# Six Winograd pairs instead of five per down projection, with two of four weight sums made by accumulating DMAs

## The chip, the cores and the metric

The kernel runs on one core of a Trainium2 chip. The metric is device time in microseconds, of one launch that does the whole computation; the median of several runs counts. TensorE (PE) multiplies, VectorE (DVE) and ScalarE (ACT) prepare operands and do the pointwise work, GpSimd (POOL) does little, and SyncE (SP) only issues DMAs.

## The reference, cut to what matters

The model is a two-layer trunk over 256 tokens of width 1024, all in float32. Each layer is a feed-forward block (FFN), a mixer and a second FFN, each followed by a residual and a layer norm, so four FFNs in all. The change sits in the FFN:

```python
def swiglu(x, w_gu, w_down):
    g, u = jnp.split(x @ w_gu, 2, axis=-1)          # 1024 -> 2 x 2816
    return (jax.nn.silu(g) * u) @ w_down            # 2816 -> 1024
...
x = layer_norm(ALPHA * x + 0.5 * swiglu(x, w_gu, w_down), g, b)
```

The hidden width 2816 is 22 chunks of 128. The down projection is therefore a sum of 22 products, each of a 256x128 piece of the hidden state and 128 rows of `w_down`.

## The kernel before, in words

**Precision.** Every float32 operand is split into a rounded part (`hi`) and a remainder (`lo`); a product is three matmuls (`mm3`, lines 169 to 171): hi*hi, hi*lo, lo*hi. The split is one copy on ACT (line 141) and one subtraction on DVE (line 142).

**Weight stream.** All weights come as one list `W` of tiles of 128x1024 floats (512 KB), in the order of use. SP loads them in that order into `raw`, a ring of RAW = 5 buffers (`w_dma`). `refill` splits the next tile when the ring of RING = 8 hi/lo slots has room, and then issues one more load; a slot comes free when the last matmul that reads it is done (`w_done`). So the load of tile n+5 waits until tile n is split, and the split of a tile waits for a slot that PE frees. SP issues in program order; on the other engines a scheduler orders the instructions at build time, by priority and by its own estimate of when operands are there.

**The FFN.** Up to eight tiles ("groups") and then, chunk by chunk, a `gate` and an `up` tile give the hidden state: `chunk(c)` makes silu(gate)*up in PSUM banks of tag `m` (three buffers) and splits the result. A plain hidden chunk is multiplied at the end by its `down` tile in `out_proj` (24 matmuls of 512 columns for two chunks). Ten of the chunks (C0 = 4 and on, NP = 5 pairs) go another way: two chunks, two token halves and two column halves make a 2x2 block product, which a Strassen-Winograd scheme does in seven products instead of eight. For output half r and pair p, `pair(r, p)` does these seven (21 matmuls of 256 columns) into four PSUM accumulators of tag `a`; `fold(r)` combines the four into the residual `xn` when the last pair of the half is done. The scheme needs sums of hidden blocks (`hs`, lines 407 to 410) and four sums of weight blocks (`tt`), which DVE makes from the raw tile in `refill` (lines 124, 126, 127) before they are split like a weight tile. A pair tile takes two slots.

**Order.** `SLOTS` says after which chunk a pair comes. With five pairs, half r = 0 comes after chunks 7, 9, 11, 13 and 15, and r = 1 after chunks 16, 17, 18, 19 and 20; then chunk 21, then `out_proj` with 12 plain down tiles. `out_proj` takes its four accumulators from tag `a`, does the first five chunks for both token halves and the last seven in a skewed order, so that the layer norm of token half 0 runs beside the matmuls of half 1.

**The rest.** The layer norm's gain and bias lie in a buffer `gb` of their own, which `load_gb` fills on SP when the layer norm before has used it up. Intermediates live in `page`, a pool of PAGES = 30 buffers of 516 floats.

Of the kernel before, what the change touches and what calls it, by code (L numbers as in the profile page):

```python
# [11 lines left out]
OP = mybir.AluOpType  # L12
# [10 lines left out]
EPS = 1e-5  # L23
RING = 8
RAW = 5
PAGES = 30
NP = 5
C0 = 4
NWARM = 7
TT = 2  # L30


PAIRS = range(C0, C0 + 2 * NP, 2)
# [1 line left out]
SLOTS = {}  # L35
for _p in range(NP):
    SLOTS.setdefault(C0 + 2 * _p + 3, []).append((0, _p))
    SLOTS.setdefault(C0 + 2 * NP + 2 + _p, []).append((1, _p))


def ffn_plan(head):
# [8 lines left out]
def trunk(ctx, tc, W, F_d, x_d, g_d, b_d, rope_d, id_d, idb_d, mk_d, tri_d, sel_d,  # L50
# [16 lines left out]
    def bank_a(shape=(P, 512)):  # L67
        return bank("a", 4, shape)
# [18 lines left out]
    def small(name, shape):  # L87
        return spool.tile(list(shape), F32, tag=name, name=name)

    raw, whi, wlo = {}, {}, {}  # L90
    stream = {}
    for n0, head in ((0, 1), (94, 2), (160, 2), (258, 2)):
        for i, e in enumerate(ffn_plan(head)):
# [7 lines left out]
    def w_dma():  # L101
        n = ring["dma"]
        if n < NG:
            raw[n] = wpool.tile([P, 1024], F32, tag="raw", name="raw", bufs=RAW)
            nc.sync.dma_start(out=raw[n], in_=W[n - 4])
            ring["dma"] = n + 1

    def slot():
        ring["free"] -= 1
# [3 lines left out]
    def refill():  # L113
        while ring["split"] < NG and ring["free"] >= (2 if paired(ring["split"]) else 1):
            n = ring["split"]
            ring["split"] = n + 1
            r = raw.pop(n)
            hi, lo = slot()
            if paired(n):
                yh, yl = slot()  # L120
                tt = wpool.tile([P, 4, 256], F32, tag="tt", name="tt", bufs=TT)
                bb = r.rearrange("p (a n) -> p a n", a=4)
                sub = nc.vector.tensor_tensor
                sub(out=tt[:, 0:2, :], in0=bb[:, 0:1, :].to_broadcast([P, 2, 256]), in1=bb[:, 1:3, :], op=OP.subtract)
                split(r[:, 256:1024], hi[:, 0:768], lo[:, 0:768])
                sub(out=tt[:, 2, :], in0=bb[:, 2, :], in1=tt[:, 0, :], op=OP.subtract)
                sub(out=tt[:, 3, :], in0=bb[:, 3, :], in1=tt[:, 2, :], op=OP.subtract)
                split(tt.rearrange("p a n -> p (a n)"), yh, yl)
                whi[n], wlo[n] = (hi, yh), (lo, yl)
            else:  # L130
                split(r, hi, lo)
                whi[n], wlo[n] = hi, lo
            w_dma()
# [39 lines left out]
    xTh = cpool.tile([P, KC, S], F32R, name="xTh")  # L173
    xTl = cpool.tile([P, KC, S], F32R, name="xTl")
    xn = cpool.tile([P, 2, D], F32, name="xn")
    gb = cpool.tile([P, 2, D], F32, name="gb")
    ident = cpool.tile([P, P], F32, name="ident")
    identb = cpool.tile([P, P], BF, name="identb")
    maskb = cpool.tile([P, 2, P], BF, name="maskb")
# [18 lines left out]
                                               ap=[[0, P], [1, width]]))  # L198

    def load_gb(k):  # L200
        bcast(gb[:, 0, :], g_d, k, D)
        bcast(gb[:, 1, :], b_d, k, D)

    st = {}

# [30 lines left out]
            nc.sync.dma_start(out=ident, in_=id_d)  # L236
    refill()
    nc.sync.dma_start(out=xn, in_=x_d)
    load_gb(0)

    def load_consts():
        nc.sync.dma_start(out=identb, in_=idb_d)
# [9 lines left out]
        nc.gpsimd.tensor_tensor(out=r, in0=r, in1=half[:, :width], op=OP.pow)  # L252
        return r

    def layer_norm(t, acc, scale, eps, k, last=False, segs=((0, 512), (512, 512))):
        st = small("lnst", [P, 3, 6])
        mv = small("lnmv", [P, 2])
        for i, (o, w) in enumerate(segs):
            if i < 2:
                sl = xn[:, t, i * 512:(i + 1) * 512]  # L260
                if scale is None:
                    nc.vector.tensor_tensor(out=sl, in0=sl, in1=acc[i], op=OP.add)
                else:
                    nc.vector.scalar_tensor_tensor(out=sl, in0=sl, scalar=scale, in1=acc[i], op0=OP.mult, op1=OP.add)
            else:
                sl = xn[:, t, o:o + w]
                nc.vector.tensor_tensor(out=sl, in0=sl, in1=acc[2][:, 0:w], op=OP.add)
            nc.vector.bn_stats(out=st[:, i, :], in_=xn[:, t, o:o + w])
            yield 1 + min(i, 1)
        nc.vector.bn_aggr(out=mv, in_=st[:, 0:len(segs), :])  # L270
        rs = rstd_of(mv[:, 1:2], eps, "lnrs")
        for h in range(2):
            sl = xn[:, t, h * 512:(h + 1) * 512]
            nc.vector.scalar_tensor_tensor(out=sl, in0=sl, scalar=mv[:, 0:1], in1=gb[:, 0, h * 512:(h + 1) * 512],
                                           op0=OP.subtract, op1=OP.mult)
        for h in range(2):
            sl = xn[:, t, h * 512:(h + 1) * 512]
            nc.vector.scalar_tensor_tensor(out=sl, in0=sl, scalar=rs, in1=gb[:, 1, h * 512:(h + 1) * 512],
                                           op0=OP.mult, op1=OP.add)
            yield 1  # L280
            if last:
                nc.sync.dma_start(out=out_d[t * P:(t + 1) * P, h * 512:(h + 1) * 512], in_=sl)
            else:
                pt = bank_a((P, 4, P))
                for c in range(4):
                    nc.tensor.transpose(pt[:, c, :], sl[:, c * P:(c + 1) * P], ident)  # L286
                o = (slice(None), slice(4 * h, 4 * h + 4), slice(t * P, (t + 1) * P))
                split(pt, xTh[o], xTl[o])
            yield 1
        if t == 1 and k + 1 < 6:  # L290
            load_gb(k + 1)

    pending = []

# [21 lines left out]
        w_done(n)  # L316
        tick()

    def out_proj(nk, n0, lhs, skew, k, scale, eps, last):
        acc = [[None, None], [None, None]]  # L320

        def one(c, t, release, hs=(0, 1)):
            n = n0 + c
            lh, ll = lhs(c, t)
            for h in hs:
                if acc[t][h] is None:
                    acc[t][h] = bank_a()
            for h in hs:
                mm3(acc[t][h], lh, ll, whi[n][:, h * 512:(h + 1) * 512], wlo[n][:, h * 512:(h + 1) * 512],
                    c == 0, c == nk - 1)  # L330
            if release:
                w_done(n)
            if 1 in hs:
                tick()

        for c in range(nk - skew):
            one(c, 0, False)
            one(c, 1, True)
        for c in range(nk - skew, nk):
            one(c, 0, False, (0,))  # L340
        ln0 = layer_norm(0, acc[0], scale, eps, k, last)
        next(ln0)
        for c in range(nk - skew, nk):
            one(c, 0, False, (1,))
        spawn(ln0)
        if last:
            segs = ((0, 512), (512, 256), (768, 256))
            accs = [acc[1][0], acc[1][1], bank_m()]
            ln1 = layer_norm(1, accs, scale, eps, k, last, segs)
            for i, (o, w) in enumerate(segs):  # L350
                for c in range(nk - skew, nk):
                    n = n0 + c
                    lh, ll = lhs(c, 1)
                    mm3(accs[i][:, 0:w], lh, ll, whi[n][:, o:o + w], wlo[n][:, o:o + w],
                        i == 2 and c == nk - skew, c == nk - 1)
                next(ln1)
            finish(ln0)
            return spawn(ln1)
        for c in range(nk - skew, nk):
            one(c, 1, True)  # L360
        finish(ln0)
        return spawn(layer_norm(1, acc[1], scale, eps, k, last))

    def ffn(n0, k, ln_prev, last=False):
        hT, hS, acc = {}, {}, {}
# [17 lines left out]
        def chunk(c):  # L383
# [20 lines left out]
                                    op=OP.mult)  # L404
            if o == 1:
                tt = nc.vector.tensor_tensor
                tt(out=hs[:, 4, :], in0=hs[:, 0, :], in1=hs[:, 2, :], op=OP.add)
                tt(out=hs[:, 5, :], in0=hs[:, 4, :], in1=hs[:, 1, :], op=OP.subtract)
                tt(out=hs[:, 6, :], in0=hs[:, 0, :], in1=hs[:, 1, :], op=OP.subtract)
                tt(out=hs[:, 7, :], in0=hs[:, 3, :], in1=hs[:, 5, :], op=OP.subtract)  # L410
                for lo, hi in ((1, 5), (5, 8)):
                    qh = page("hSh", [P, hi - lo, P], F32R)
                    ql = page("hSl", [P, hi - lo, P], F32R)
# [4 lines left out]
        def pair(r, p):  # L418
# [18 lines left out]
        def fold(r, a):  # L437
# [8 lines left out]
            tt(out=u[:, 1, :], in0=u[:, 0, :], in1=a[3][:, 0, :], op=OP.add)  # L446
            tt(out=x[:, 1, :], in0=u[:, 0, :], in1=a[1][:, 1, :], op=OP.add)
# [431 lines left out]
def _arrays(np, i):  # L879
# [5 lines left out]
    def ffn(l, f, head):  # L885
# [4 lines left out]
        for e in ffn_plan(head):  # L890
# [93 lines left out]
```

## Time and profile before

| | |
|---|---|
| median of 3 runs | 958.51 us (958.47 to 958.96) |
| the profiled execution's own time | 959.6 us |
| its span, first to last instruction | 957.9 us |
| PE / DVE / ACT / POOL busy, share of the span | 99% / 76% / 52% / 2% |
| mean granted TensorE clock | 0.998 of full |
| DMA: moved, mean rate | 183.09 MB, 191 GB/s |

The time of the profiled execution is 1.7 us more than its span, and 1.1 us more than the median. A matmul's shown duration includes the pipeline and overlaps the next one; what a matmul costs is the distance from its start to the next start.

### The profile page before, as it was taken

The page shows a single profiled execution, that of the slowest core. Times are in us where ns is not written, and L with a number is a line of the kernel's source. Part 1 is how long each engine was busy: PE and PEld are TensorE (multiplying, and loading weights), DVE is VectorE, ACT ScalarE, POOL GpSimd, SP SyncE. Part 2 cuts the span into 40 slices and gives each one's busy share as a digit, 9 for nine tenths or more (in the row PEclk, how much of TensorE's full clock was granted, in tenths as well). Part 3 has the DMA queues.
Part 4 walks back from the last instruction along what each step waited for, and adds up shares of the span by engine and source line. Part 5 has one row for each costly group of instructions (what it writes and reads, how often), then busy time and mean ns, then how long its engine had stood idle before and what let it go on. Part 6 is the DMA issues. An engine that isn't in the chain of part 4 may idle for free.

```text
span 957.9 us, 16624 instructions
## 1 busy us (share of the span) xinstructions
PE 946.4 (99%) x6586; PEld 867.2 (91%) x6586; DVE 732.5 (76%) x1125; ACT 495.6 (52%) x705; POOL 21.0 (2%) x28
## 2 busy tenths in 40 slices
PE   9999999999999999999999999999999999999997
PEld 7999998887888999998889999988888789999985
DVE  7698886685767788976878779748767887888765
ACT  6565564445645555553355555525675445555530
POOL 0000000010100000000000000001000000000000
PEclk9999999999999999999999999999999999999999
DMA  8976557474436665576565656756634366655631
GB/s 307 319 237 217 174 200 228 161 273 152 138 129 219 202 195 176 179 234 205 173 221 162 190 177 200 238 158 221 220 132 122 136 213 216 195 173 180 219 112 44
DMA packets 52077, 183.09 MB, mean 191 GB/s; under 512 B 6176, under 2 KB 6688, under 8 KB 51872
## 3 DMA queue, kind: packets, MB, share of 16 engines
q1 hardware_dynamic: 51856, 181.77, 57.6%
q8 instruction: 51, 0.84, 0.4%
q10 hardware_dynamic: 144, 0.26, 0.1%
q14 instruction: 26, 0.21, 0.1%
HBM read 180.97 MB, written 1.05 MB: 190 GB/s over the span
## 4 chain that ended last, share of the span: by engine, by line
PE 70%; DVE 2%; DMA 1%; issue 1%; ACT 1%; POOL 0%; DVEq 0%
PE ps_m L169 15%; PE ps_m L170 15%; PE ps_m L171 15%; PE ps_a L169 5%; PE ps_a L170 5%; PE ps_a L171 5%; PE ps_a L430 3%; PE ps_a L431 3%; PE ps_a L429 3%; DVE wlo L142 1%; PE ps_a L286 1%; DMA raw<-in_W 1%; ACT whi L141 0%; PE ps_t L377 0%; PE ps_a L613 0%
## 5 line engine op out<-in xcount | busy, mean ns | idle before, releaser
L141 ACT CAST whi<-raw 128x1024 fp32r<-128x1024 f32 (+2 forms) x327 | 331.0, 1016 | 258.9 <-PE ps_a L171 77.2
L142 DVE TENSOR_TENSOR wlo<-raw,whi 128x1024 fp32r<-128x1024 f32 (+2 forms) x327 | 380.9, 1176 | 89.2 <-ACT whi L141 86.4
L169 PE MATMUL ps_m<-xTh,whi 128*128 128x256 f32 x1280 | 358.8, 280 | 0.9 <-DVE qkc L760 0.9
L171 PE MATMUL ps_m<-xTh,wlo 128*128 128x256 f32 x1280 | 357.9, 280 | 0.2 <-DVE wlo L142 0.2
L170 PE MATMUL ps_m<-xTl,whi 128*128 128x256 f32 x1280 | 357.7, 279 | 0.0
L169 PEld LDWEIGHTS ps_m<-xTh,whi 128*128 128x128 f32 x1280 | 240.6, 188 | 1.5 <-issue 1.2
L170 PEld LDWEIGHTS ps_m<-xTl,whi 128*128 128x128 f32 x1280 | 240.6, 188 | 0.6 <-issue 0.3
L171 PEld LDWEIGHTS ps_m<-xTh,wlo 128*128 128x128 f32 x1280 | 240.5, 188 | 0.6 <-DVE wlo L142 0.4
L169 PE MATMUL ps_m<-whi,xTh 128*128 128x512 f32 x224 | 90.9, 406 | 0.0
L170 PE MATMUL ps_m<-wlo,xTh 128*128 128x512 f32 x224 | 89.3, 399 | 0.0
L171 PE MATMUL ps_m<-whi,xTl 128*128 128x512 f32 x224 | 88.8, 397 | 0.0
L430 PE MATMUL ps_a<-wlo,hSh 128*128 128x256 f32 x280 | 78.8, 281 | 0.0
L429 PE MATMUL ps_a<-whi,hSh 128*128 128x256 f32 x280 | 78.8, 281 | 0.0
L431 PE MATMUL ps_a<-whi,hSl 128*128 128x256 f32 x280 | 78.8, 281 | 0.0
L169 PE MATMUL ps_a<-whi,hT 128*128 128x512 f32 (+1 forms) x192 | 75.3, 392 | 0.0
L170 PE MATMUL ps_a<-wlo,hT 128*128 128x512 f32 (+1 forms) x192 | 75.0, 390 | 0.0
L171 PE MATMUL ps_a<-whi,hT 128*128 128x512 f32 (+1 forms) x192 | 74.9, 390 | 0.0
L141 ACT CAST whi<-tt 128x1024 fp32r<-128x1024 f32 x40 | 42.1, 1052 | 42.6 <-issue 18.3
L430 PEld LDWEIGHTS ps_a<-wlo,hSh 128*128 128x128 f32 x280 | 52.8, 189 | 0.0
L431 PEld LDWEIGHTS ps_a<-whi,hSl 128*128 128x128 f32 x280 | 52.8, 188 | 0.0
L429 PEld LDWEIGHTS ps_a<-whi,hSh 128*128 128x128 f32 x280 | 52.7, 188 | 0.0
L142 DVE TENSOR_TENSOR wlo<-tt,whi 128x1024 fp32r<-128x1024 f32 x40 | 48.8, 1221 | 3.4 <-ACT whi L141 3.4
(224 smaller groups left out, 1013.7 us busy)
## 6 DMA issues: line engine op xcount, KB each, us to landing
raw<-in_W SPq DMA_DIRECT2D x320, 512.0 KB, 4.4
gb<-in_g SPq DMA_DIRECT2D x6, 512.0 KB, 4.2
gb<-in_b SPq DMA_DIRECT2D x6, 512.0 KB, 5.2
raw<-in_F SPq DMA_DIRECT2D x7, 384.0 KB, 4.0
xn<-in_x SPq DMA_DIRECT2D x1, 1024.0 KB
out<-xn SPq DMA_DIRECT2D x4, 256.0 KB, 2.0
swt<-in_sw SPq DMA_DIRECT2D x2, 256.0 KB, 6.7
hg<-in_hg SPq DMA_DIRECT2D x2, 256.0 KB, 5.5
```

The costliest lines, as they stand in the source:

```text
L141: nc.scalar.copy(out=hi, in_=src)
L142: nc.vector.tensor_tensor(out=lo, in0=src, in1=hi.bitcast(F32), op=OP.subtract)
L169: mm_(out=out, lhsT=lh, rhs=rh, start=start, stop=False)
L170: mm_(out=out, lhsT=lh, rhs=rl, start=False, stop=False)
L171: mm_(out=out, lhsT=ll, rhs=rh, start=False, stop=stop)
L286: nc.tensor.transpose(pt[:, c, :], sl[:, c * P:(c + 1) * P], ident)
L429: mm_(out=o, lhsT=lh, rhs=rh, start=p == 0 and h == 0, stop=False, skip_group_check=True)
L430: mm_(out=o, lhsT=lh, rhs=rl, start=False, stop=False, skip_group_check=True)
L431: mm_(out=o, lhsT=ll, rhs=rh, start=False, stop=p == NP - 1, skip_group_check=True)
```

## The change

NP goes from 5 to 6, so two more chunks (14 and 15) leave the plain down projection: 12 pair tiles and 10 down tiles per FFN instead of 10 and 12. Half r = 0 now comes after chunks 7, 9, 11, 13, 15 and 17, and half r = 1 after 18, 19 and 20 and, three pairs in a row, after 21. The signs of the Winograd scheme are arranged anew so that two of the four weight sums are plain additions to a first block. A pair tile is no longer one load: SP loads two blocks into `tt`, SP loads three blocks into `raw`, and GpSimd issues a transfer that adds the fourth block from HBM onto both blocks in `tt`. DVE makes only the other two sums. `out_proj` of an FFN takes three accumulators from tag `m` and one from tag `t` (one buffer). The buffer `gb` goes; gain and bias lie in four pages that `out_proj` loads at its start; PAGES goes to 32 and the ring of `tt` from 2 to 3.

```diff
-PAGES = 30
-NP = 5
+PAGES = 32
+NP = 6
-TT = 2
+TT = 3
...
-    SLOTS.setdefault(C0 + 2 * NP + 2 + _p, []).append((1, _p))
+    SLOTS.setdefault(min(C0 + 2 * NP + 2 + _p, FC - 1), []).append((1, _p))
...
     def w_dma():
...
-            raw[n] = wpool.tile([P, 1024], F32, tag="raw", name="raw", bufs=RAW)
-            nc.sync.dma_start(out=raw[n], in_=W[n - 4])
             ring["dma"] = n + 1
+            r = raw[n] = wpool.tile([P, 1024], F32, tag="raw", name="raw", bufs=RAW)
+            w = W[n - 4]
+            if not paired(n):
+                nc.sync.dma_start(out=r, in_=w)
+                return
+            tt = sums[n] = wpool.tile([P, 4, 256], F32, tag="tt", name="tt", bufs=TT)
+            nc.sync.dma_start(out=tt[:, 0:2, :].rearrange("p a n -> p (a n)"), in_=w[:, 0:512])
+            nc.sync.dma_start(out=r[:, 0:768], in_=w[:, 0:768])
+            nc.gpsimd.dma_start(out=tt[:, 0:2, :], in_=w[:, None, 768:1024].to_broadcast([P, 2, 256]), accum_op=OP.add)
...
             if paired(n):
                 yh, yl = slot()
-                tt = wpool.tile([P, 4, 256], F32, tag="tt", name="tt", bufs=TT)
-                bb = r.rearrange("p (a n) -> p a n", a=4)
-                sub = nc.vector.tensor_tensor
-                sub(out=tt[:, 0:2, :], in0=bb[:, 0:1, :].to_broadcast([P, 2, 256]), in1=bb[:, 1:3, :], op=OP.subtract)
-                split(r[:, 256:1024], hi[:, 0:768], lo[:, 0:768])
-                sub(out=tt[:, 2, :], in0=bb[:, 2, :], in1=tt[:, 0, :], op=OP.subtract)
-                sub(out=tt[:, 3, :], in0=bb[:, 3, :], in1=tt[:, 2, :], op=OP.subtract)
+                tt = sums.pop(n)
+                split(r[:, 0:768], hi[:, 0:768], lo[:, 0:768])
+                add = nc.vector.tensor_tensor
+                add(out=tt[:, 2, :], in0=r[:, 256:512], in1=tt[:, 0, :], op=OP.add)
+                add(out=tt[:, 3, :], in0=r[:, 512:768], in1=tt[:, 2, :], op=OP.add)
                 split(tt.rearrange("p a n -> p (a n)"), yh, yl)
...
     def load_gb(k):
-        bcast(gb[:, 0, :], g_d, k, D)
-        bcast(gb[:, 1, :], b_d, k, D)
+        gb = {}
+        for h in range(2):
+            for j, d in enumerate((g_d, b_d)):
+                v = gb[j, h] = page("gb", [P, 512])
+                nc.sync.dma_start(out=v, in_=bass.AP(tensor=d.tensor, offset=d.offset + k * D + h * 512,
+                                                     ap=[[0, P], [1, 512]]))
+        return gb
...
-        if t == 1 and k + 1 < 6:
-            load_gb(k + 1)
...
     def out_proj(nk, n0, lhs, skew, k, scale, eps, last, banks=None):
         acc = [[None, None], [None, None]]
+        gb = load_gb(k)
+        if banks is None:
+            banks = {(t, h): bank_a for t in range(2) for h in range(2)}
...
-                tt(out=hs[:, 4, :], in0=hs[:, 0, :], in1=hs[:, 2, :], op=OP.add)
-                tt(out=hs[:, 5, :], in0=hs[:, 4, :], in1=hs[:, 1, :], op=OP.subtract)
-                tt(out=hs[:, 6, :], in0=hs[:, 0, :], in1=hs[:, 1, :], op=OP.subtract)
-                tt(out=hs[:, 7, :], in0=hs[:, 3, :], in1=hs[:, 5, :], op=OP.subtract)
+                tt(out=hs[:, 4:6, :], in0=hs[:, 0:1, :].to_broadcast([P, 2, P]), in1=hs[:, 1:3, :], op=OP.subtract)
+                tt(out=hs[:, 6, :], in0=hs[:, 5, :], in1=hs[:, 1, :], op=OP.subtract)
+                tt(out=hs[:, 7, :], in0=hs[:, 3, :], in1=hs[:, 6, :], op=OP.add)
...
-        return out_proj(len(PLAIN), at["down", PLAIN[0]], lhs, 7, k, None, 4.0 * EPS, last)
+        return out_proj(len(PLAIN), at["down", PLAIN[0]], lhs, 7, k, None, 4.0 * EPS, last,
+                        {(0, 0): bank_m, (0, 1): bank_m, (1, 0): bank_m, (1, 1): bank_t})
```

In `pair` three of the seven products take other weight columns, and `fold` makes its sums with the new signs, the last addition to token half 0 as two instructions of 256 columns instead of one of 512.

## Rows read from the trace of the kernel before

**Rows 1.** The page: busy time by engine, and the chain by engine.
```profile
PE 946.4 (99%) x6586; PEld 867.2 (91%) x6586; DVE 732.5 (76%) x1125; ACT 495.6 (52%) x705; POOL 21.0 (2%) x28
...
PE 70%; DVE 2%; DMA 1%; issue 1%; ACT 1%; POOL 0%; DVEq 0%
```
**Rows 2.** PE's own waits: total us, times, longest us.
```profile
PE ps_t L194 <- DVE wz L191: 1.3, 1, 1.3
PE ps_m L169 <- DVE qkc L760: 0.9, 1, 0.9
PE ps_t L377 <- DVE hp L373: 0.5, 1, 0.5
```
**Rows 3.** PE timeline, second FFN: start, duration; one pair, first and last.
```profile
360.84 0.28 PE L429 MATMUL ps_a<-whi,hSh 128*128 128x256 f32 x1
...
363.25 0.28 PE L431 MATMUL ps_a<-whi,hSl 128*128 128x256 f32 x1
363.36 0.28 PE L169 MATMUL ps_m<-xTh,whi 128*128 128x256 f32 x1
```
**Rows 4.** PE timeline, second FFN: its 135 down matmuls before the first transpose.
```profile
436.94 0.40 PE L169 MATMUL ps_a<-whi,hT 128*128 128x512 f32 x1
...
468.10 0.40 PE L171 MATMUL ps_a<-whi,hT 128*128 128x512 f32 x1
468.34 0.49 PE L286 MATMUL ps_a<-ident,xn 128*128 128x128 f32 x3
```
**Rows 5.** Groups by line and form: count, busy us, mean ns.
```profile
L142 DVE TENSOR_TENSOR wlo<-raw,whi 128x1024 fp32r<-128x1024 f32 x280 | 338.3, 1220 | 77.5 <-ACT whi L141 75.2
L142 DVE TENSOR_TENSOR wlo<-tt,whi 128x1024 fp32r<-128x1024 f32 x40 | 48.8, 1221 | 3.4 <-ACT whi L141 3.4
L142 DVE TENSOR_TENSOR wlo<-raw,whi 128x768 fp32r<-128x768 f32 x40 | 38.1, 952 | 11.3 <-ACT whi L141 11.3
L124 DVE TENSOR_TENSOR tt<-raw 128x512 f32<-128x512 f32 x40 | 27.5, 687 | 24.0 <-DMA raw<-in_W 24.0
L127 DVE TENSOR_TENSOR tt<-raw,tt 128x256 f32<-128x256 f32 x40 | 16.9, 422 | 0.8
L142 DVE TENSOR_TENSOR hSl<-hs,hSh 128x512 fp32r<-128x512 f32 x20 | 13.7, 683 | 0.0
```
**Rows 6.** Stretches: r = 0 pairs, r = 1 pairs, down projection, the start.
```profile
335.85:388.25 52.40, 52.40 (x449) 52.40 (x448) 43.10 (x67) 28.08 (x39) 0.00 (x0) 1.00 0.59 185
388.25:431.33 43.08, 43.08 (x368) 43.08 (x367) 35.26 (x49) 25.54 (x35) 0.00 (x0) 1.00 0.63 208
436.94:468.34 31.40, 31.40 (x138) 25.32 (x136) 18.14 (x23) 11.32 (x12) 0.92 (x1) 1.00 0.45 147
3.00:23.74 20.74, 20.30 (x114) 16.72 (x112) 16.43 (x27) 14.18 (x25) 0.00 (x0) 1.00 0.99 341
```
**Rows 7.** SP, DVE and PE timelines: one r = 1 pair, load to use.
```profile
405.71 0.33 SPq L105 DMA_DIRECT2D raw<-in_W  x1
...
415.32 0.95 DVE L142 TENSOR_TENSOR wlo<-raw,whi 128x768 fp32r<-128x768 f32 x1
416.49 1.22 DVE L142 TENSOR_TENSOR wlo<-tt,whi 128x1024 fp32r<-128x1024 f32 x1 [0.23 <-ACT whi L141]
...
428.84 0.28 PE L429 MATMUL ps_a<-whi,hSh 128*128 128x256 f32 x1
```
**Rows 8.** Page, DMA issues: KB each, median us from issue to landing.
```profile
raw<-in_W SPq DMA_DIRECT2D x320, 512.0 KB, 4.4
out<-xn SPq DMA_DIRECT2D x4, 256.0 KB, 2.0
sel<-in_sel SPq DMA_DIRECT2D x1, 256.0 KB, 7.4
```
**Rows 9.** GpSimd's timeline, one of its two operations on a 128x512 tile.
```profile
201.10 1.10 POOL L504 TENSOR_SCALAR_AFFINE_SELECT swt<-swt 128x512 f32<-128x512 f32 x1 [5.08 <-DMA swt<-in_sw]
```
**Rows 10.** DVE timeline: the fold of r = 0; PE's next use of the banks.
```profile
391.81 0.41 DVE L445 TENSOR_TENSOR fu<-fx,ps_a 128x256 f32<-128x256 f32 x1
...
393.94 0.68 DVE L449 SCALAR_TENSOR_TENSOR xn<-xn,ps_a 128x512 f32<-128x512 f32 x1
394.53 0.68 DVE L450 SCALAR_TENSOR_TENSOR xn<-xn,ps_a 128x512 f32<-128x512 f32 x1
...
396.35 0.29 PE L429 MATMUL ps_a<-whi,hSh 128*128 128x256 f32 x1
```

More of the change, by code (lines that the diff above doesn't have):

```diff
@@ L88, in small @@
         return spool.tile(list(shape), F32, tag=name, name=name)
-    raw, whi, wlo = {}, {}, {}
+    raw, sums, whi, wlo = {}, {}, {}, {}
     stream = {}
@@ L175, in trunk @@
     xn = cpool.tile([P, 2, D], F32, name="xn")
-    gb = cpool.tile([P, 2, D], F32, name="gb")
     ident = cpool.tile([P, P], F32, name="ident")
@@ L253, in rstd_of, with layer_norm @@
         return r
-    def layer_norm(t, acc, scale, eps, k, last=False, segs=((0, 512), (512, 512))):
+    def layer_norm(t, acc, gb, scale, eps, k, last=False, segs=((0, 512), (512, 512))):
         st = small("lnst", [P, 3, 6])
@@ L273, in layer_norm @@
             sl = xn[:, t, h * 512:(h + 1) * 512]
-            nc.vector.scalar_tensor_tensor(out=sl, in0=sl, scalar=mv[:, 0:1], in1=gb[:, 0, h * 512:(h + 1) * 512],
+            nc.vector.scalar_tensor_tensor(out=sl, in0=sl, scalar=mv[:, 0:1], in1=gb[0, h],
                                            op0=OP.subtract, op1=OP.mult)
@@ L277, in layer_norm @@
             sl = xn[:, t, h * 512:(h + 1) * 512]
-            nc.vector.scalar_tensor_tensor(out=sl, in0=sl, scalar=rs, in1=gb[:, 1, h * 512:(h + 1) * 512],
+            nc.vector.scalar_tensor_tensor(out=sl, in0=sl, scalar=rs, in1=gb[1, h],
                                            op0=OP.mult, op1=OP.add)
@@ L317, in proj_t, with out_proj @@
         tick()
-    def out_proj(nk, n0, lhs, skew, k, scale, eps, last):
+    def out_proj(nk, n0, lhs, skew, k, scale, eps, last, banks=None):
         acc = [[None, None], [None, None]]
+        gb = load_gb(k)
+        if banks is None:
+            banks = {(t, h): bank_a for t in range(2) for h in range(2)}
         def one(c, t, release, hs=(0, 1)):
@@ L326, in one @@
                 if acc[t][h] is None:
-                    acc[t][h] = bank_a()
+                    acc[t][h] = banks[t, h]()
             for h in hs:
@@ L340, in out_proj @@
             one(c, 0, False, (0,))
-        ln0 = layer_norm(0, acc[0], scale, eps, k, last)
+        ln0 = layer_norm(0, acc[0], gb, scale, eps, k, last)
         next(ln0)
@@ L347, in out_proj @@
             segs = ((0, 512), (512, 256), (768, 256))
-            accs = [acc[1][0], acc[1][1], bank_m()]
-            ln1 = layer_norm(1, accs, scale, eps, k, last, segs)
+            accs = [acc[1][0], acc[1][1], bank_a()]
+            ln1 = layer_norm(1, accs, gb, scale, eps, k, last, segs)
             for i, (o, w) in enumerate(segs):
@@ L361, in out_proj @@
         finish(ln0)
-        return spawn(layer_norm(1, acc[1], scale, eps, k, last))
+        return spawn(layer_norm(1, acc[1], gb, scale, eps, k, last))
     def ffn(n0, k, ln_prev, last=False):
@@ L423, in pair @@
             for i, half, col, b, h in ((1, 0, 0, 2, 0), (3, 0, 2, 0, 0), (7, 0, 1, 0, 1), (2, 1, 3, 1, 0),
-                                       (4, 1, 0, 1, 1), (5, 1, 2, 2, 1), (6, 1, 1, 3, 0)):
+                                       (4, 1, 1, 1, 1), (6, 1, 2, 2, 1), (5, 1, 0, 3, 0)):
                 w = slice(256 * col, 256 * col + 256)
@@ L445, in fold @@
             tt(out=u[:, 0, :], in0=x[:, 0, :], in1=a[2][:, 1, :], op=OP.add)
-            tt(out=u[:, 1, :], in0=u[:, 0, :], in1=a[3][:, 0, :], op=OP.add)
-            tt(out=x[:, 1, :], in0=u[:, 0, :], in1=a[1][:, 1, :], op=OP.add)
+            tt(out=x[:, 1, :], in0=a[3][:, 0, :], in1=u[:, 0, :], op=OP.subtract)
+            tt(out=u[:, 1, :], in0=u[:, 0, :], in1=a[1][:, 1, :], op=OP.subtract)
             stt = nc.vector.scalar_tensor_tensor
@@ L450, in fold @@
             stt(out=x1, in0=x1, scalar=2.0 * ALPHA, in1=a[0], op0=OP.mult, op1=OP.add)
-            tt(out=x0, in0=x0, in1=u[:, 1:2, :].to_broadcast([P, 2, 256]), op=OP.add)
             tt(out=x1, in0=x1, in1=x, op=OP.add)
+            tt(out=x0[:, 0, :], in0=x0[:, 0, :], in1=u[:, 1, :], op=OP.add)
+            tt(out=x0[:, 1, :], in0=x0[:, 1, :], in1=x[:, 1, :], op=OP.add)
         if ln_prev is None:
@@ L898, in ffn @@
                 o, q = 2 * e[1], C0 + 2 * e[2]
-                v = np.concatenate([wd[q][:, o + 1], wd[q][:, o], wd[q + 1][:, o + 1], wd[q + 1][:, o]], axis=1)
+                v = np.concatenate([wd[q][:, o], wd[q + 1][:, o + 1], wd[q + 1][:, o], wd[q][:, o + 1]], axis=1)
             parts.append(v[None])
```

1 line of the change is left out of this document (removed).

## The prediction

> **What bounds the kernel now.** I read the page first. PE is busy 99% of the span and the chain that ended last is PE for 70%, with no other engine above 2% [rows 1]. PE's own waits say the same from the other side: the three longest add up to 2.7 us, and all three lie outside the FFN's pairs and down projections [rows 2]. So time changes by what PE has to do, or by a new wait of PE, and by nothing else. Work that leaves DVE or ACT earns nothing by itself.
>
> What a matmul costs is read from starts, not from durations. A pair is 21 matmuls of 256 columns from 360.84 to the next start at 363.36: 2.52 us, 0.120 each [rows 3]. It ran at the upper of the two clock levels, as the stretches show (1.00) [rows 6]. The 135 down matmuls of 512 columns before the first transpose run from 436.94 to 468.34: 31.40 us, 0.2326 each [rows 4].
>
> **What the change takes from PE.** Two chunks leave the plain down projection in each FFN: 2 chunks x 2 token halves x 2 column halves x 3 = 24 matmuls, 24 x 0.2326 = 5.58 us. They come back as one more pair for each half r: 2 x 2.52 = 5.04 us. That is 0.54 us per FFN; the r = 1 stretch holds six pairs and five chunks of 48 matmuls [rows 6], so a chunk is (43.08 - 6 x 2.5)/5 = 5.6 us, 0.117 per start, and a pair at that rate would cost 2.45, so 0.54 to 0.68 us. Four FFNs: 2.2 to 2.7 us; I take 2.3. Gate and up matmuls, mixers and transposes stay.
>
> **What it does to DVE.** Removed per pair tile: one sum of 512 columns (0.687) and two of 256 (0.42 each), 1.53 us; added two of 256, 0.84 us [rows 5]; 0.69 us less for each tile. The splits of a pair tile stay (0.95 + 1.22). Per FFN: 12 tiles x 3.01 against 10 x 3.70 is -0.9; two down tiles less, -2.4; one more hidden pair with its sums and splits against two plain hidden chunks, about +0.6; two folds with an addition cut in two (0.41 x 2 against 0.68), +0.3. So DVE loses 2.4 us of work per FFN. DVE's share in the r = 1 stretch is 35.26 of 43.08 us [rows 6], so this is cover, not gain. ACT gets two more tiles of two copies each in place of two of one; it is busy 52%.
>
> **What it does to the transfers.** A pair tile was one load of 512 KB. It becomes 256 + 384 KB on SP and 256 KB on GpSimd, 896 KB. In the r = 1 stretch a period is one chunk and one pair, 5.60 + 2.50 = 8.1 us, with 1024 + 896 KB: 242 GB/s, against 208 at a DMA share of 0.63 now and 341 at 0.99 at the start [rows 6]. If the adding transfer also reads its destination through the same engines it is 274. Both fit. Chunk 21 with its three pairs wants 3.8 MB in 13.1 us, 290 GB/s (350 with the reads): the queue is full there, for 13 us, and the lead below covers it.
>
> **The new chain.** The sum is two transfers, one behind the other: `tt` must land, GpSimd sees it, issues, and the sum must land. DVE wants it after the first split of the tile. Now the load of an r = 1 pair is issued at 405.71, its split of 768 columns ends at 416.27, and PE uses the tile at 428.84 [rows 7]. So the chain has 10.6 us for nothing, and 12.3 us more from the second split's start until PE needs the tile. The trace has no adding transfer and no DMA from GpSimd. Bounds from the nearest rows: a transfer of 256 KB takes 2.0 us from issue to landing where the queue was empty and 7.4 where it was full; a raw tile 4.4 [rows 8]. GpSimd's own part lies between nothing and the 1.1 us of one of its operations on a 512-column tile [rows 9]. The chain is then 2.0 + 0 + 2.0 = 4.0 us at least and 7.4 + 1.1 + 7.4 = 15.9 at most. I take the raw tile's 4.4 twice, because these transfers run in the same half-full queue and the adding one does more per byte, and 1.1: 9.9 us, hidden by 0.7 us, and nothing on PE.
>
> The Trainium skill (DMA: Bandwidth & Descriptors, Anatomy of one DMA — SWDGE (gpsimd) path) gives a GpSimd transfer about 2.0 us fixed plus its bytes at 436 GB/s, from which I estimate 2.6 us for 256 KB, and it says nothing there of adding; the chain would be 4.4 + 1.1 + 2.6 = 8.1 us, with the same result. The same page (Latency and other measured facts) speaks against the change in that it gives the GpSimd path a later first byte, about 1 us against 0.6; no run here has shown that yet.
>
> Queued behind the waiting GpSimd instruction are only the next sum and the layer norm's power of -0.5, which comes once pairs are over. Behind a DVE sum that waits are the gate product of the next chunk and the fold. On SP nothing waits for GpSimd directly, but `raw` comes free only after the two DVE sums, so a late sum delays the load of tile n+5 by as much.
>
> **Costed at nothing, with their cover.** Gain and bias move from the end of one layer norm to the start of `out_proj`: the same bytes, in a stretch with a DMA share of 0.45 [rows 6], needed after 3 x 2.8 + 14 x 0.7 = 18 us of matmuls in an FFN. If their pages aren't free, the weight loads behind them on SP wait; up to thirteen tiles are on their way by then, over 25 us of PE work. The accumulators of `out_proj` in tags `m` and `t`: PE last used `m` before the three pairs, 7.5 us earlier, so silu and product have emptied them; the next stage needs them one projection later. The ring: three pairs in a row hold six of eight slots, so the last four down tiles get slots only when the last pair ends. They are 4 x 1.22 us on DVE, with the fold between (3 x 0.41 + 3 x 0.68 + 2 x 0.41 = 4.1 us by [rows 5, 10]), 9 us; the tenth tile is wanted 3 x 2.8 + 6 x 0.7 = 12.6 us after that. It fits by 3.6 us.
>
> **The sum.** Against its own execution, 959.6 - 2.3 = 957.3; that execution lies 1.1 us above the median, so the median becomes 956.2 us. With 2.2 to 2.7, and up to 0.4 us of small waits, 955.8 to 956.7. A difference under 0.2%, 1.9 us, is about what a measurement of this kernel can't tell from no change.
>
> **Rivals.**
>
> *The fold waits (same).* Half r = 1 reuses the four accumulators that the fold of r = 0 empties. Now DVE's last reads end at 394.6 and 395.2, and PE comes at 396.35 [rows 10]: a margin of 1.1 us. If the chain takes 12 to 12.7 us instead of 9.9, a sum in DVE's queue ahead of the fold is 1.4 to 2.1 us late, and PE waits 0.3 to 1.0 us in each FFN, 1 to 4 us in all: 957.4 to 960.2. For it: DVE waited for plain raw tiles already, 24.0 us in front of line 124 [rows 5]. Against it: DVE has 0.69 us less to do per tile.
>
> *Late sums everywhere (slower).* In the r = 1 stretch DVE has (43.08 - 35.26)/43.08 x 8.1 = 1.5 us idle per period [rows 6], 2.2 with the relief, and in r = 0 (52.40 - 43.10)/52.40 x 13.7 + 0.69 = 3.1. A chain of 15.9 us is 5.3 late at each of 12 pairs: 6 x (5.3 - 2.2) + 6 x (5.3 - 3.1) = 31.8 us per FFN, 12.3 of it paid by the lead, 19.5 left on PE, 78 us in four: 1034. It decides from about 13 us on, where the fold already costs 4 x 1.3 us: 961 and up. For it: both transfers share the queue with the tile's other load. Against it: 13 us needs both near the worst that rows 8 show.
>
> *The gain is lost at the end (same).* If DVE enters `out_proj` more than 3.6 us late, PE waits for the last down tiles, about 0.5 us per FFN for each 0.5 us; 2 us in all gives 958.
>
> **Chances.** Forecast 0.48, fold 0.20, late sums 0.25, lost at the end 0.07. Faster by over 0.2% is the forecast without its upper edge, 0.46; same is fold, end and that edge, 0.29; slower 0.25. The forecast's own range is 955.8 to 956.7. The range for 8 in 10 takes in fold and end and the nearer third of the late sums, and 0.3 us below for a cheaper pair: 955.5 to 966.
>
> **What the profile after would show.** Right: 48 pairs of about 2.5 us; PE still without waits in the FFNs; the sums' wait on DVE no longer than its wait in front of line 124 now; the adding transfer from issue to landing under 6 us. Wrong: PE waiting on DVE at the first matmul of pair (1, 0) is the fold; PE waiting for `wlo` along r = 1 and the three pairs is the late sums; waiting in `out_proj` is the end. What would make it wrong at once is a GpSimd transfer that takes more than 7 us, or one whose issue holds GpSimd for several.

## The result, and the profile after

The changed kernel takes 1029.21 us (median of 6 runs, 1023.31 to 1035.64) against 958.98 us before (6 runs, 958.47 to 960.15). The ratio is 1.073 [1.070, 1.076]: 7.3% slower, where 956.2 us were forecast and 966 was the top of the range. The profiled execution took 1035.64 us, the longest of the six; its span is 1033.9.

The page of the changed kernel: busy time by engine, the chain that ended last by engine and by line, three groups of instructions and GpSimd's transfer, and the DMA issues with their median time from issue to landing.

```profile
PE 970.0 (94%) x6658; PEld 885.1 (86%) x6658; DVE 717.8 (69%) x1109; ACT 494.5 (48%) x713; POOL 79.0 (8%) x76
...
PE 23%; DMA 18%; DVE 10%; issue 5%; ACT 2%; SPq 0%; DVEq 0%; POOL 0%; ACTq 0%; POOLq 0%
DMA tt<-in_W 16%; PE ps_m L175 6%; PE ps_m L174 6%; PE ps_m L176 6%; DVE wlo L147 5%; DMA raw<-in_W 2%; ACT whi L146 2%; DVE tt L131 1%; PE ps_a L175 1%; PE ps_a L176 1%; PE ps_a L174 1%; PE ps_a L294 1%; DVE hp L401 0%; PE ps_a L439 0%; PE ps_a L438 0%
...
L174 PE MATMUL ps_m<-xTh,whi 128*128 128x256 f32 x1280 | 367.4, 287 | 45.1 <-DVE hs L412 29.8
...
L131 DVE TENSOR_TENSOR tt<-raw,tt 128x256 f32<-128x256 f32 x48 | 20.4, 425 | 198.8 <-DMA tt<-in_W 190.4
...
L146 ACT CAST whi<-tt 128x1024 fp32r<-128x1024 f32 x48 | 50.2, 1046 | 121.5 <-DVE tt L132 108.1
L113 POOL DMA_DIRECT2D tt<-in_W x48 | 58.0, 1208 | 554.7 <-DMA tt<-in_W 293.7
...
raw<-in_W SPq DMA_DIRECT2D x272, 512.0 KB, 4.9
...
tt<-in_W SPq DMA_DIRECT2D x48, 256.0 KB, 5.3
tt<-in_W POOLq DMA_DIRECT2D x48, 256.0 KB, 6.8
```

Before, the chain was PE for 70% [rows 1]. Now 16% of it is the transfers into `tt` alone. DVE stands 198.8 us in front of line 131, the first sum that it makes itself; that is the place that answers to line 124, which had 24.0 us [rows 5]. DVE's work fell (717.8 against 732.5 us); its share fell more, from 76% to 69%, because the span grew by 76.0 us.

The waits of the changed kernel: engine, line, what it waited for; us in total, times, longest us.

```profile
DVE tt L131 <- DMA tt<-in_W: 190.4, 35, 7.8
...
PE ps_m L174 <- DVE hs L412: 29.8, 14, 3.3
PE ps_m L174 <- ACT hp L397: 9.0, 9, 1.9
...
PE ps_m L175 <- DVE wlo L147: 6.2, 7, 2.0
...
PE ps_m L174 <- DVE hp L401: 5.3, 4, 2.4
...
PE ps_a L437 <- DVE fx L454: 2.5, 3, 0.8
```

What PE lacks is hardly ever a split weight (6.2 us). It is a PSUM bank of tag `m` (29.8 + 9.0 + 5.3 = 44.1 us). For 35.1 us of that, the gate product of a chunk (lines 401 and 412) is queued on DVE behind a sum that waits, so the bank isn't emptied. For the other 9.0 us it is ACT's silu (line 397), and ACT comes late too: it stands 108.1 us in front of its copies of `tt` until DVE's second sum is made (line 132). One such place in the second FFN, from SP's, GpSimd's, DVE's and PE's timelines (start, duration, in brackets the idle time before it and what ended it):

```profile
384.81 0.42 SPq L111 DMA_DIRECT2D tt<-in_W  x1
...
391.27 1.20 POOL L113 DMA_DIRECT2D tt<-in_W  x1 [15.74 <-DVE wlo L147]
...
396.97 0.28 PE L439 MATMUL ps_a<-whi,hSl 128*128 128x256 f32 x1
397.32 0.42 DVE L131 TENSOR_TENSOR tt<-raw,tt 128x256 f32<-128x256 f32 x1 [6.26 <-DMA tt<-in_W]
397.78 0.42 DVE L132 TENSOR_TENSOR tt<-raw,tt 128x256 f32<-128x256 f32 x1
398.12 1.22 DVE L147 TENSOR_TENSOR wlo<-raw,whi 128x1024 fp32r<-128x1024 f32 x1
399.26 0.41 DVE L412 TENSOR_TENSOR hs<-hp,ps_m 128x256 f32<-128x256 f32 x1
...
399.73 0.38 PE L174 MATMUL ps_m<-xTh,whi 128*128 128x256 f32 x1 [2.47 <-DVE hs L412]
...
400.73 0.95 DVE L147 TENSOR_TENSOR wlo<-raw,whi 128x768 fp32r<-128x768 f32 x1
```

The first load of the tile is issued at 384.81, the sum has landed by 397.32: a chain of 12.5 us. DVE came to line 131 at 391.06 (397.32 - 6.26), 6.3 us after the load. The tile's own subtraction of 768 columns, which the prediction put ahead of the sums, starts at 400.73, behind them and behind another tile's split, the gate product and one more split. PE goes on as soon as that product is done.

Worked out over all 48 tiles from the same rows and the transfers' landings (median): load of two blocks 5.35 us, from its landing to GpSimd's issue 0.57, GpSimd's transfer 6.79 from issue to landing; the whole chain 12.9 (8.0 to 15.1). DVE is free for the sum 8.3 us after the load's issue (6.3 for r = 0, 10.2 for r = 1); the subtraction of 768 columns ends 18.0 us after it. The sum stands ahead of that subtraction in 42 of the 48 tiles.

PE's idle time explains part of the loss only: PE is also busy longer, although it has the matmuls of a kernel (e1, below) in which they take 943.6 us. Windows of the changed kernel around one gap: busy us of PE, PEld, DVE, ACT and POOL, then the granted clock, the DMA share and GB/s.

```profile
86.00:95.00 9.00, 9.00 (x80) 9.00 (x78) 3.05 (x4) 4.30 (x7) 1.20 (x1) 1.00 0.77 208
95.00:98.20 3.20, 0.25 (x3) 0.04 (x1) 2.04 (x4) 1.03 (x1) 0.00 (x0) 1.00 0.07 10
98.20:101.60 3.40, 3.06 (x14) 3.07 (x15) 3.33 (x7) 0.30 (x2) 0.00 (x0) 0.50 0.70 196
101.60:105.00 3.40, 3.40 (x31) 3.40 (x30) 3.40 (x6) 3.40 (x5) 0.00 (x0) 1.00 0.82 279
```

After PE stood for 3.2 us, the granted clock is 0.50 (the lower of the two levels, 1.2 GHz) for 3.4 us and then 1.00 again; 14 matmuls run in the slow window, 31 in the next. The trace has ten such stretches before the last matmuls, 37.4 us in all.

### The profile page after: what moved, and what is told of

Read it like the earlier page. It is cut to its first block, busy times and chain, and to the rows that moved or that the text cites. A ratio compares the mean times of both kernels' runs of the same rounds, so it can differ in the third digit from the quotient of the medians.

```text
span 1033.9 us, 17043 instructions
## 1 busy us (share of the span) xinstructions
PE 970.0 (94%) x6658; PEld 885.1 (86%) x6658; DVE 717.8 (69%) x1109; ACT 494.5 (48%) x713; POOL 79.0 (8%) x76
## 3 DMA queue, kind: packets, MB, share of 16 engines
q0 software_dynamic: 13056, 12.59, 8.1%
## 4 chain that ended last, share of the span: by engine, by line
PE 23%; DMA 18%; DVE 10%; issue 5%; ACT 2%; SPq 0%; DVEq 0%; POOL 0%; ACTq 0%; POOLq 0%
DMA tt<-in_W 16%; PE ps_m L175 6%; PE ps_m L174 6%; PE ps_m L176 6%; DVE wlo L147 5%; DMA raw<-in_W 2%; ACT whi L146 2%; DVE tt L131 1%; PE ps_a L175 1%; PE ps_a L176 1%; PE ps_a L174 1%; PE ps_a L294 1%; DVE hp L401 0%; PE ps_a L439 0%; PE ps_a L438 0%
## 5 line engine op out<-in xcount | busy, mean ns | idle before, releaser
L174 PE MATMUL ps_m<-xTh,whi 128*128 128x256 f32 x1280 | 367.4, 287 | 45.1 <-DVE hs L412 29.8
L131 DVE TENSOR_TENSOR tt<-raw,tt 128x256 f32<-128x256 f32 x48 | 20.4, 425 | 198.8 <-DMA tt<-in_W 190.4
L146 ACT CAST whi<-tt 128x1024 fp32r<-128x1024 f32 x48 | 50.2, 1046 | 121.5 <-DVE tt L132 108.1
L113 POOL DMA_DIRECT2D tt<-in_W x48 | 58.0, 1208 | 554.7 <-DMA tt<-in_W 293.7
L437 PE MATMUL ps_a<-whi,hSh 128*128 128x256 f32 x336 | 95.0, 283 | 2.7 <-DVE fx L454 2.5
L438 PE MATMUL ps_a<-wlo,hSh 128*128 128x256 f32 x336 | 94.3, 281 | 0.0
L439 PE MATMUL ps_a<-whi,hSl 128*128 128x256 f32 x336 | 94.2, 280 | 0.0
L437 PEld LDWEIGHTS ps_a<-whi,hSh 128*128 128x128 f32 x336 | 63.2, 188 | 3.8 <-DVE fx L454 3.2
L146 ACT CAST hSh<-hs 128x512 fp32r<-128x512 f32 (+1 forms) x48 | 27.1, 565 | 77.2 <-DVE hs L416 74.0
L439 PEld LDWEIGHTS ps_a<-whi,hSl 128*128 128x128 f32 x336 | 63.3, 188 | 0.0
L438 PEld LDWEIGHTS ps_a<-wlo,hSh 128*128 128x128 f32 x336 | 63.3, 188 | 0.0
L147 DVE TENSOR_TENSOR wlo<-tt,whi 128x1024 fp32r<-128x1024 f32 x48 | 58.5, 1219 | 4.2 <-ACT whi L146 4.2
```

Source lines behind the costliest of these rows:

```text
L113: nc.gpsimd.dma_start(out=tt[:, 0:2, :], in_=w[:, None, 768:1024].to_broadcast([P, 2, 256]), accum_op=OP.add)
L131: add(out=tt[:, 2, :], in0=r[:, 256:512], in1=tt[:, 0, :], op=OP.add)
L146: nc.scalar.copy(out=hi, in_=src)
L147: nc.vector.tensor_tensor(out=lo, in0=src, in1=hi.bitcast(F32), op=OP.subtract)
L174: mm_(out=out, lhsT=lh, rhs=rh, start=start, stop=False)
L437: mm_(out=o, lhsT=lh, rhs=rh, start=p == 0 and h == 0, stop=False, skip_group_check=True)
```

## The experiments

Two readings were to be told apart. **Place and lateness:** the sums stand early in DVE's queue, the chain ends later than DVE gets there, and everything behind them waits. **Rivals:** the 20 MB more that are moved; the rest of the edit (sixth pair, banks, pages); GpSimd's transfer as such. e1 to e4 ran on one chip (before 958.94 us there), e5 to e8 on another (959.37), e9 to e11 on a third (959.23). The diffs are against the changed kernel and shortened (`...`); what stands behind a `#` in them is a comment.

**e1: the change with one load for each tile and all four sums on DVE.**

```diff
-            tt = sums[n] = wpool.tile(...)         # three transfers
+            nc.sync.dma_start(out=r, in_=w)        # one load of 512 KB
...
+                add(out=tt[:, 0:2, :], in0=r[:, 0:512].rearrange("p (a n) -> p a n", a=2),
+                    in1=r[:, None, 768:1024].to_broadcast([P, 2, 256]), op=OP.add)
```

> Six pairs, all else of the change kept, but a pair tile is one load of 512 KB again and DVE makes all four sums (one of 512 columns, two of 256). Late-sum theory (DVE's queue stands at the first sum until two transfers in series have landed, 12.9 us in the median, and PE waits for an m bank whose gate product is queued behind it): 955.5 to 957.5 us, the 2.2 to 2.7 us of the sixth pair and no new wait. Traffic theory (19 MB more on the DMA engines make all loads late): the same, since the bytes go back to 183 MB. Structure theory (the sixth pair, three pairs in a row, the banks and pages of out_proj): it stays above 1000.

Measured: 956.02 us (955.37 to 956.12), ratio 0.9968 [0.9956, 0.998]. Busy time on its page:

```profile
PE 943.6 (99%) x6658; PEld 869.4 (91%) x6658; DVE 752.3 (79%) x1157; ACT 505.5 (53%) x713; POOL 20.7 (2%) x28
```

Its wait at the sums, now for `raw`:

```profile
DVE tt L124 <- DMA raw<-in_W: 19.6, 18, 2.2
```

So sixth pair, new signs, banks and pages lose nothing; the whole loss comes with the transfers. Against this kernel the changed one's span is 79.6 us longer: PE idle 63.9 against 10.7 (+53.2), PE busy 970.0 against 943.6 (+26.4). At half the clock, the 37.4 us of slow stretches cost at most 18.7 us of that; taken from start to start, the matmuls in them took about 16 us longer. Most of the rest stands at the edges of the gaps: the last matmul before one counts with its whole 0.28 us, where its cost is 0.12 [rows 3], and the first after one with 0.38 (timeline above).

**e2: the change with five pairs.**

```diff
-NP = 6
+NP = 5
```

> The changed kernel with NP back to 5: no sixth pair, no three pairs in a row, adding transfers kept for 40 pair tiles. Late-sum theory: ten of twelve waits per FFN stay, 958.5 + 70 x 10/12, about 1017 (1005 to 1025), DVE's wait at the first sum about 150 to 170 us. Traffic theory: nearly the same, 15.7 of 18.9 MB more remain, about 1015. Structure theory: 958 to 962.

Measured: 1011.99 us (one run). DVE's wait at the sums:

```profile
DVE tt L131 <- DMA tt<-in_W: 153.4, 31, 7.9
```

The loss is there without the sixth pair, and without three pairs in a row. Traffic and late sums forecast nearly the same here, so this run doesn't tell them apart.

**e3: the two sums held behind the tile's own subtraction of 768 columns.** All transfers stay.

```diff
-                split(r[:, 0:768], hi[:, 0:768], lo[:, 0:768])
+                first = split(r[:, 0:768], hi[:, 0:768], lo[:, 0:768])
...
+                with tc.issue_after(first.ins):
                     add(out=tt[:, 2, :], ...)
                     add(out=tt[:, 3, :], ...)
```

> The changed kernel; the two DVE sums are queued on DVE behind the tile's own 768-column subtraction instead of several instructions ahead of it. Same transfers, same bytes. Late-sum theory: the sum is wanted about 10.6 us after its load is issued instead of about 6.5, so a chain of 12.9 us is 2 to 3 us late instead of 6 to 7, which DVE's idle time nearly covers: 957 to 975, DVE's wait at the first sum 50 to 120 us instead of 190. Traffic theory: no change, 1015 to 1035. Structure theory: no change.

Measured: 957.05 us (956.09 to 959.13), ratio 0.9981 [0.9972, 0.999]. DVE now comes to the sums 14.7 us (median) after the load instead of 8.3; the chain is 12.4. That is later than the 10.6 us of the expectation, and the wait is below the 50 to 120 us expected:

```profile
DVE tt L132 <- DMA tt<-in_W: 22.0, 7, 6.5
```

DVE's timeline in the second FFN, with the new order:

```profile
387.12 0.96 DVE L148 TENSOR_TENSOR wlo<-raw,whi 128x768 fp32r<-128x768 f32 x1 [1.39 <-ACT whi L147]
388.00 0.42 DVE L132 TENSOR_TENSOR tt<-raw,tt 128x256 f32<-128x256 f32 x1
388.45 0.42 DVE L133 TENSOR_TENSOR tt<-raw,tt 128x256 f32<-128x256 f32 x1
```

With the same bytes and nearly the same chain, 72 of the 73 us are gone by moving two instructions on one queue. This alone brings down the rivals of traffic and of GpSimd as such.

**e4: the two transfers of a sum issued two tiles earlier**, the sums left where they were (a fourth `tt` buffer; the zeros `wz` share another tile to make room).

```diff
-TT = 3
+TT = 4
...
     def w_dma():
         n = ring["dma"]
+        for m in range(n, n + 3):
+            sum_dma(m)                 # SP load into tt, then GpSimd's transfer
```

> The changed kernel, but tt has four buffers and the two transfers of a sum are issued two tiles before the load of its tile's raw part; place of the sums on DVE almost as in the changed kernel, same bytes. To make room, the zeros of the warm-up matmuls are an existing tile of zeros. Late-sum theory: the chain gets about 5 us more (two tiles of 2.7 us), DVE's wait at the first sum falls under 40 us and the time to 956 to 962. Traffic theory: all bytes are still there, 1010 or more. Structure theory: 1015 or more.

Measured: 964.58 us (962.88 to 968.12), ratio 1.0065 [1.005, 1.0079]. DVE's waits at the sums and, last, PE's longest wait:

```profile
DVE tt L139 <- DMA tt<-in_W: 38.9, 15, 5.5
...
DVE tt L139 <- DMA raw<-in_W: 17.6, 10, 3.8
...
PE ps_t L393 <- DVE hp L389: 6.4, 3, 2.5
```

An earlier start takes away most of the loss too, though the time stays 2.6 us above the range expected: the wait at the sums for `tt` goes from 190.4 to 38.9 us. PE's named wait lies at the start of the three later FFNs, where the first pair's sum stands ahead of the group's product. 8.6 us more than e1 stay.

**e5: GpSimd copies the block over `tt` instead of adding it** (the addition is left out). DVE's order and the two transfers in series stay.

```diff
-... in_=w[:, None, 768:1024].to_broadcast([P, 2, 256]), accum_op=OP.add)
+... in_=w[:, None, 768:1024].to_broadcast([P, 2, 256]))
```

> The changed kernel, except that GpSimd's transfer copies the fourth block over both blocks of tt instead of adding it (the addition is left out of the computation). Bytes, the two transfers in series and DVE's order stay. Theory A (two transfers in series, wanted too early in DVE's queue): the copy lands about as late as the adding transfer did (6.8 us after its issue), the chain stays at 12 to 13 us, DVE waits about 190 us at the sums, and the time is 1005 to 1036. Rival B (adding makes the transfer slow, the read of the destination): the copy lands within 4 us, the chain is 9 to 10 us, DVE's wait falls below 80 us and the time below 985.

Measured: 969.42 us (one run). The time is the one that rival B expected (below 985); the landing (4.9 us), the chain (11.2) and the wait lie between the two expectations. The wait at the sums:

```profile
DVE tt L131 <- DMA tt<-in_W: 128.8, 37, 6.3
```

On its page, GpSimd's instruction and the landing of its transfer:

```profile
L113 POOL DMA_DIRECT2D tt<-in_W x48 | 34.9, 727 | 522.8 <-DMA tt<-in_W 268.8
...
tt<-in_W POOLq DMA_DIRECT2D x48, 256.0 KB, 4.9
```

Adding costs 1.9 us of landing (6.8 against 4.9); GpSimd's own instruction is 0.48 us longer (1.21 against 0.73). The chain's median goes from 12.9 to 11.2. That is still late 37 times, as theory A, the series, wants, but the time falls much further than that theory expected: 60 us for 1.7 us of chain. So the price isn't proportional to the wait; see below.

**e6: no load into `tt` at all, GpSimd only copies** (first blocks and addition are left out): one transfer instead of two in series.

```diff
-            nc.sync.dma_start(out=tt[:, 0:2, :]..., in_=w[:, 0:512])
```

> The changed kernel without the load of two blocks into tt, and GpSimd's transfer copies the fourth block there (first blocks and addition are left out of the computation). DVE's order and GpSimd's part stay; one transfer in place of two in series. Theory A (the series): the sum can run about 7 us after the tile's load is issued, DVE comes to it after about 8, so its wait at the sums falls from 190 to under 30 us and the time to 957 to 965. Rival B (GpSimd's own transfer, its issue or its landing under load, is enough to be late): the transfer still lands 8 us or more after the issue of the tile's load, DVE waits over 80 us and the time stays above 980.

Measured: 958.38 us (one run). DVE's longest wait at the sums is now for `raw`:

```profile
DVE tt L130 <- DMA raw<-in_W: 14.6, 18, 1.7
```

GpSimd's transfer on its page, landed 3.3 us after its issue:

```profile
tt<-in_W POOLq DMA_DIRECT2D x48, 256.0 KB, 3.3
```

So copying transfers from GpSimd cost little where they start early (958.38 against e1's 956.02, on another chip). But the run does not test what it was meant to: with no load of SP's to wait for, GpSimd issues the copy as soon as a `tt` buffer is free, in the median 19 us before SP issues the tile's own load, and in 44 of 48 tiles before it. That one transfer issued together with the tile's load would be in time is argued from the parts of the chain, not shown.

**e7: e3 and e4 together.**

> Both remedies together: the transfers of a sum are issued two tiles ahead of the tile's own load, and DVE makes the sums behind the tile's subtraction of 768 columns. If what the later place alone left over (957.05 against 956.02 with all sums on DVE) is lateness, DVE's waits at the sums (22 us there) go below 8 us and the time to 955.8 to 956.4. Rival: what is left is the price of the 20 MB more that are moved, or of the early transfers in the way of other loads: 956.8 to 958, with DVE's and PE's waits in front of raw tiles in place of those at the sums.

Measured: 955.99 us (955.72 to 956.38), ratio 0.9967 [0.9954, 0.9979]. Of the wait at the sums for `tt`, 0.6 us is left: DVE now comes to them 20.5 us (median) after the load of `tt`, at a chain of 11.2. So what e3 left over was lateness, not traffic.

**e8: e1 with five pairs.**

> Everything of the change except the sixth pair and the accumulating transfers: five pairs, one load of 512 KB for each tile, all four sums on DVE with the new signs, gain and bias in pages, the accumulators of the down projection in the other banks. If the sixth pair is the whole gain of 2.9 us that the kernel with six pairs and DVE's sums showed (24 matmuls of 512 columns against 42 of 256 in each FFN, 2.2 to 2.7 us): 958.4 to 959.3, the same as before within 0.05%. Rival: the new banks or pages bring part of it: 956.5 to 957.8; or they cost something that the pair pays back: 959.5 or more.

Measured: 958.01 us (957.56 to 958.57), ratio 0.9986 [0.9977, 0.9995]: neither expectation quite. To read the sixth pair's worth, the kernels of e1, e8 and e7 ran once more, beside each other.

**e9, e10, e11: the kernels of e1, e8 and e7 again.**

> The kernel with six pairs and all four sums on DVE once more, beside the one with five pairs, on one chip, so that their difference can be read. By the prediction's sum the sixth pair is worth 2.2 to 2.7 us in four FFNs: this time is lower by that much than that of the kernel with five pairs run beside it. Rival: by the two earlier calls, each against its own run of before, the pair brings 1.8 us and the other edits 1.3; then the difference here is 1.5 to 2.0.

> Five pairs, all four sums on DVE, with the new signs, pages and banks. If these edits are worth nothing, its ratio to before has 1 inside its interval, or misses it by less than 0.05%; if they bring the 1.3 us that the earlier call showed, the ratio is 0.9986 again.

> Accumulating transfers, issued two tiles earlier, sums behind the subtraction of 768 columns. If transfers that come in time relieve DVE but not the end (PE is the bound), it equals the kernel with six pairs and all sums on DVE within 0.05%; if DVE's relief still buys something on PE, it is lower by 0.5 us or more; if the 20 MB cost something, higher by 0.5 us or more.

Measured: 956.30 us (ratio 0.9964 [0.9951, 0.9976]), 958.02 (0.9985 [0.9976, 0.9993]) and 956.07 (0.9965 [0.9951, 0.9978]). The sixth pair is worth 958.02 - 956.30 = 1.7 us in medians, as the rival in e9's expectation has it and below the prediction's 2.2 to 2.7. (The profiled spans differ by 2.3, 956.9 against 954.6, but e10's is that of its longest run.) The other edits bring 959.23 - 958.02 = 1.2 us. Transfers that come in time and all sums on DVE give the same within 0.03%: taking 24 us of work off DVE (752.3 to 728.2 us busy) and moving 20 MB more buys nothing and costs nothing.

## Why the prediction was wrong, point by point

**What it had right.** PE is the bound, and the sixth pair pays: six pairs without the accumulating transfers take 956.02 and 956.30 us, where the sum gave 956.2. That closeness is partly luck: the pair measured 1.7 us by medians where 2.2 to 2.7 were taken, and the edits costed at nothing bring 1.2. Banks, pages, ring and the end of the down projection cost nothing, as said; the fold shows as 2.5 us of PE's waits, within the 1 to 4 us that its rival forecast and small beside the loss. The extra bytes fit.

**The step that failed.** "DVE wants it after the first split of the tile", and with it the 10.6 us of cover. The step took the place of the sums from the program text. DVE's queue has its own order, fixed by a scheduler at build time, and that order put the sums ahead of the tile's subtraction of 768 columns: DVE is there 8.3 us after the load, not 10.6. The trace of before could have warned. In the stretch of [rows 7], between the lines shown there, DVE's timeline of the kernel before has two sums of the same tile:

```profile
409.51 0.68 DVE L124 TENSOR_TENSOR tt<-raw 128x512 f32<-128x512 f32 x1
410.23 0.42 DVE L126 TENSOR_TENSOR tt<-raw,tt 128x256 f32<-128x256 f32 x1
```

Line 124 stands ahead of the split in the program text too, but line 126, like the sums that DVE keeps, stands behind it there. Yet it runs 4.5 us after the load at 405.71 and 5.1 us ahead of the split at 415.32, and so it does in 33 of the 40 pair tiles of before, in the median 7.2 us after the load. The 10.6 us were also one tile's: over the 40 tiles the split of 768 columns ends 8.7 to 17.0 us after the load, 12.4 in the median. e3 is the proof that the place decides: with the order that the prediction assumed, the loss is gone, at a chain of 12.4 us, though DVE comes to the sums later there (14.7 us) than the prediction had it.

**The chain was mis-sized as well.** Forecast 4.4 + 1.1 + 4.4 = 9.9 us, measured 5.35 + 0.57 + 6.79, median of the whole 12.9: inside the bounds of 4.0 and 15.9, and 3 us above the value taken. The adding transfer was priced like a raw tile; e5 and e6 show what its 6.8 us are made of: a plain copy from GpSimd takes 3.3 us where no load into `tt` goes in front of it (it also starts at other times there), 4.9 behind one, and the addition 1.9 more. The Trainium skill (DMA: Bandwidth & Descriptors, Anatomy of one DMA — SWDGE (gpsimd) path) led to an estimate of 2.6 us; e6's plain copy comes near it with 3.3, the adding one is far from it. Of a later first byte no run here gives a separate reading. By estimate, either error alone would have cost little: a 9.9 us chain is 1.6 us late at 8.3, which the prediction's slack of DVE of 2.2 and 3.1 us for each pair covers, and a chain of 12.9 is 2.3 us late at 10.6. No run has either alone: e5, at 11.2 and DVE's early place, loses 13.4 us, and in e3 DVE comes at 14.7, not at 10.6. Together they are 4.6 us late.

**The lead didn't pay.** The rival *late sums everywhere* had the mechanism, and the changed kernel is this rival. But it let a lead of 12.3 us on the weights pay the first part in each FFN, and put the point of decision at 13 us of chain. The prediction named the gate product as what is queued behind a late sum, and then counted as if PE would miss weights. PE misses banks of tag `m`, of which there are three, and waits 44.1 us for them against 6.2 for weights. Without the lead, the rival's own slack comes near the loss. The idle time in front of line 131, added up by output half over the trace's rows, less 3.1 us for each pair of r = 0 and 2.2 for each of r = 1, against the profiled time over that of the same kernel with all sums on DVE (956.0 for six pairs, 958.0 for five):

| kernel | r = 0 | r = 1 | less slack | time lost |
|---|---|---|---|---|
| changed | 133.4 - 24 x 3.1 | 65.4 - 24 x 2.2 | 71.6 us | 79.6 us |
| e2, five pairs | 103.6 - 20 x 3.1 | 57.9 - 20 x 2.2 | 55.5 us | 54.0 us |
| e5, copy | 91.3 - 24 x 3.1 | 39.3 - 24 x 2.2, below 0 | 16.9 us | 13.4 us |

That is why 1.7 us less of chain took 60 us away: in e5 the wait is 2.7 us for a pair, just about DVE's slack; in the changed kernel it is 4.1. The agreement is of totals of one execution each, and six executions of the changed kernel differ by up to 12 us; part of the time lost in the first row is the lower clock, which the count of waits doesn't hold. That the slack is exactly this is argued, not shown. e4's waits are below the slack in total and it still loses 8.6 us, because they are concentrated at the starts of FFNs; there the count by totals fails.

**The signs it named.** "Over 7 us" for GpSimd's transfer was not reached by its median (6.8) and the kernel is slow all the same; the limit of 6 us for "right" was the better one. "PE waiting for `wlo`" was named as the mark of late sums; the mark is PE waiting for `m`, ended by DVE's product (35.1 us) or ACT's silu (9.0).

**Open.** Whether a single transfer from GpSimd, issued together with the tile's load, would be in time. Why five pairs with the other edits are 1.2 us faster than before: compared matmul by matmul, the two traces drift apart by about 1 us over the whole span, with no wait that accounts for it. And what in the adding transfer takes the 1.9 us.

## What to carry to other kernels

Before a wait is moved onto a transfer, read in the trace where the waiting instruction stands in its engine's queue, not where the program text has it; and for what is queued behind it, count the cover that its own readers have (here three PSUM banks), not the cover of the data that is late. A chain of two transfers in series has to be priced as a load landing under the kernel's own traffic, twice, and more for one that adds. If such a sum is wanted, issue it tiles ahead and pin its reader late in the queue (e7); but here DVE had the time, and the same kernel with the sums left on DVE is as fast and simpler (e1 956.0, e7 956.0, before 958.9 to 959.4).

## What the runs showed of the hardware

- For the same 12.59 MB, the adding transfers are 13056 packets on GpSimd's queue and the copying ones 3840. The queue's row on the page of the changed kernel (packets, MB, share of 16 engines):

```profile
q0 software_dynamic: 13056, 12.59, 8.1%
```

The same row of e5:

```profile
q0 software_dynamic: 3840, 12.59, 3.8%
```

- GpSimd is held 1.21 us by issuing an adding transfer and 0.73 us by a copying one (e5), and in the changed kernel it issues 0.57 us (median) after the transfer it waits for has landed.
- PE's gaps cost twice: of the 79.6 us between the profiled spans, 53.2 are idle time and about 16 are matmuls that ran at the lower clock level after a gap (granted clock 0.50 for 37.4 us). The other 10 us of longer busy time stand mostly at the edges of the gaps. e5 has gaps and no such stretch before the last 3 us of its span, and PE is busy 3.6 us longer than in e1 (947.2 against 943.6).
